# Latent scores wholly in row tiles: nine rounds of four 32-row products for four key tiles, instead of one such round and eight full products

## The chip, the cores and the metric

The kernel runs on one core of a Trainium2 chip. The metric is the time of one execution on the device in microseconds (us). The core has TensorE (PE, its weight loads shown apart as PEld), VectorE (DVE), ScalarE (ACT), GpSimd (POOL) and SyncE (SP), which issues nearly all DMAs here. Each engine takes its instructions in the order in which the program lists them for it.

## The reference

One layer of a transformer, 2048 positions of width 1024, all in float32, one sequence:

```python
z = rms_norm(x) @ w_in                       # q_A, k_A, v_A, c_q, c_kv, k_rope
o_A = windowed attention (8 heads of 64, 2 kv heads, |i-j| <= 128, bias, sink)
# latent attention, 8 heads, all 2048 keys:
q = rms_norm(c_q) @ w_qb                     # per head 64 plain + 32 rotary columns
k, v = rms_norm(c_kv) @ w_kvb                # per head 64 plain columns of k, 64 of v
s = (einsum('bqhd,bkhd->bhqk', qn, k_nope)
     + einsum('bqhr,bkr->bhqk', qr, k_rot)) * scale      # k_rot is shared by all heads
o_B = softmax(s) @ v
x = x + concat(rms_norm(o_A), rms_norm(o_B)) @ w_o
x = x + expert_choice_ffn(rms_norm(x))       # 16 experts, 256 rows each, 3 matrices of 1024 x 1024
```

The change concerns `s` of the latent attention: per head a product over 64 + 32 = 96 rows.

## The kernel before, in words

The program has three regions. Region 1 projects the rows, norms and rotates them and writes queries and keys transposed into DRAM (`qT`, `kT`), each as two parts: a value rounded to the short form that TensorE takes in one pass, and the rest. Region 2 is the attention, region 3 the output projection, the router and the experts.

A score is the sum of three part products, high x high, high x rest and rest x high, so 3 x 96 = 288 rows. Before, that is laid out as two full products of 128 rows (256 rows: `kk[:, 0]` and `kk[:, 1]`, filled by `fetch_k`, L325) and one product of 32 rows for what is left, which is the rotary part that all heads share (`kr`, filled by `fetch_kr`, L337). Four of these 32-row products, for four key tiles, go to the four row groups of the array at once (`rotary`, L1113): that is the one round of before. The queries are laid out to match in `qq` of three slabs (`fetch_qq`, L345).

Region 2 runs over 8 heads, 4 chunks of 512 queries per head, and 4 groups of four key tiles per chunk: `head` (L1097). In each group one round and eight full products write four PSUM banks, two `sb` pairs out of three. ScalarE takes the exponential of each pair into `pp` (L1130, four buffers), VectorE adds it to a sum (L1133, L1135), and two value products per pair, for the two column halves of the array, add to `pv` (L1140). A value step is the two products of one pair. The windowed attention of 16 row tiles is mixed into the same queues: scores at L1004, bias add at L1009, exponential at L1012, values at L1021, denominators at L1043. Its queries come by `fetch_q` (L314), its keys by `fetch_ka` (L319).

The order of each engine's instructions is made when the program is built. Each operation has a cost, needs and a priority; a planner (`Plan.schedule`, L147) runs through them and puts the ready one with the lowest priority next. Priorities are a base plus an offset by stage and engine, the table `OFF2` for region 2. For TensorE it prefers, within 4.0, an operation of the array mode it is in: "r" for row groups, "c" for column halves, none for the full array. Every load is one operation of SP with cost 0.5 (`load`, L409), however many DMAs its function issues; its bytes are counted at 230 KB per us. Keys of the next head and queries of the next chunk are fetched into second buffers. A DMA reuses one of eight semaphores in turn, so it waits until the DMA eight before it has landed. At the end of region 1 SP issues what the start of region 2 needs: the bias table, the windows' first tiles, the first queries (`qq0`) and the first eight key tiles of head 0 (`PRE_K`).

Of the kernel before, what the change touches and what calls it, by code (L numbers as in the profile page):

```python
# [46 lines left out]
OFF2 = {'bfP': -89.2, 'aG': -6.5, 'awV': -1.5, 'bfS': -57.7, 'bfV': 89.2, 'asP': -33.4, 'awP': -84.8, 'bfA': -1.0, 'bfG': -6.1, 'bvP': 29.3, 'awS': -37.9, 'avP': 28.4, 'afS': 47.0, 'blS': -30.5, 'bV': 10.7, 'pfS': 58.5}  # L47
# [211 lines left out]
def build(tc, nc, a, out, dbg=None, upto=9, path="both"):  # L259
# [35 lines left out]
    class Views:  # L295


        def __init__(self):
# [4 lines left out]
            self.qq0 = carve(3, 512)  # L303
            self.va = f(carve(4, 2, 64))
            self.qs = [carve(8, P), None]
            self.kr = carve(4, P)
            v0, k0 = f(carve(NT, VD)), carve(2, SEQ)
            self.free = WB[:, carve.used[0]:]
            v1, k1 = f(carve(NT, VD)), carve(2, SEQ)
# [15 lines left out]
        def fetch_k(self, h, c0, c1):  # L325

            kk, src = f(self.kk[h % 2]), kT[h // 4, :, h % 4]
            cs = slice(c0, c1)
# [106 lines left out]
    def region1():  # L435
        with ExitStack() as st:
# [401 lines left out]
            if PRE_K:  # L838
                pl.load(P * 6144, V2.fetch_qq(0, 0, lambda: V2.qq0), sum((KT[t] for t in range(4)), [MK]), [], pr=PRE_PR + 1)
                pl.load(P * 8 * PRE_K * P, V2.fetch_k(0, 0, PRE_K * P), sum((KT[t] for t in range(PRE_K)), [MK]), [], pr=PRE_PR + 2)  # L840
                pl.load(P * 512 * PRE_K // 4, V2.fetch_kr(0, PRE_K // 4), sum((KT[t] for t in range(PRE_K)), [MK]), [], pr=PRE_PR + 2)
# [20 lines left out]
    def region2(mix):  # L862
# [3 lines left out]
        with ExitStack() as st:  # L866
# [211 lines left out]
            def latent():  # L1078
                vts = [pl.fixed(b) for b in V2.vts]
                KR = pl.fixed(V2.kr)  # L1080
                pl.home.update({("kk", i): V2.kk[i] for i in range(2)})
                pl.home[("qq", 0)] = V2.qq0
                for h in range(8):
                    pl.prio, pl.stage = 64 * h - 20, "bl"
                    kk = pl.buf(wk, [P, 2, SEQ], F32R, "kk", 2)
                    vt = vts[h % 2]
                    cuts = [PRE_K, NT] if h == 0 else [0, 8, NT]
                    if h == 0:
                        kk.slot, kk.t = 0, V2.kk[0]
                        pl.load(P * 512, V2.fetch_kr(PRE_K // 4, 4), [], [(KR, m) for m in range(PRE_K // 4, 4)])  # L1090
                    for c0, c1 in zip(cuts, cuts[1:]):
                        pl.load(P * 1024 * (c1 - c0), V2.fetch_k(h, c0 * P, c1 * P), [], [(kk, kt) for kt in range(c0, c1)])
                        pl.load((c1 - c0) << 15, V2.fetch_v(h, c0, c1), [], [(vt, kt) for kt in range(c0, c1)])
                    for qc in range(4):
                        head(h, qc, kk, vt, KR)

            def head(h, qc, kk, vt, KR):  # L1097
                qsl = slice(qc * 512, qc * 512 + 512)
                pl.prio, pl.stage = 64 * h + 16 * qc - 20, "bl"
                qq = pl.buf(wk, [P, 3, 512], F32R, "qq", 2)  # L1100
                if h + qc == 0:
                    qq.slot, qq.t = 0, V2.qq0
                else:
                    pl.load(P * 6144, V2.fetch_qq(h, qc, qq), [], [qq])
# [3 lines left out]
                for m in range(4):  # L1108
# [636 lines left out]
```

## Time and profile before

| | |
|---|---|
| median of 3 runs | 2641.65 us (2641.4 to 2643.09) |
| profiled execution | 2643.56 us, span of its instructions 2641.8 us |
| mean granted TensorE clock | 0.967 |
| region 2 on TensorE | from 491.58 us (first window scores) to 1220.5 us; output projection from 1229.29 us |
| TensorE, VectorE, ScalarE busy | 94%, 62%, 46% of the span |

The profile lists instructions by line of the program, engine and operation, with the tile they write and the tiles they read. A matmul's record begins when it enters the array; ends are modelled and overlap, so the pace is read from one start to the next. Time in which an engine waits stands behind a row in brackets, with what ended it. A DMA's row on SP is its issue; its data land later.

### The profile page before, as it was taken

How to read it: one execution, taken by the hardware profiler on the slowest of the kernel's cores; microseconds unless marked ns; L12 is line 12 of the kernel's file. 1: busy time of each engine (PE TensorE's matmuls, PEld its weight loads, DVE VectorE, ACT ScalarE, POOL GpSimd, SP SyncE). 2: the span in 40 equal slices, each digit the busy share in tenths (PEclk: the TensorE clock that was granted, in tenths of full speed). 3: DMA queues.
4: the chain of work that ended last, by engine and by line, in shares of the span. 5: the costliest groups of instructions: out<-in, count | busy, mean ns of one | idle time of the engine just before them, and what ended most of it. 6: DMA issues, size and time to landing. Idle time of an engine off the chain costs nothing.

```text
span 2641.8 us, 38721 instructions
## 1 busy us (share of the span) xinstructions
PE 2479.2 (94%) x15002; PEld 1975.9 (75%) x15002; DVE 1645.4 (62%) x3022; ACT 1204.5 (46%) x1731; POOL 343.1 (13%) x284
## 2 busy tenths in 40 slices
PE   6599999699999999998999499999999999999997
PEld 5599999444444444444888399999999999999996
DVE  6366665486768677667767775555555555555552
ACT  5254444344444444444444244545544544554442
POOL 2132333111211111000000000000000000000000
PEclk8799999799999999999999599999999999999999
DMA  5434443864424432314544156666666666666662
GB/s 186 83 110 116 127 113 111 207 158 103 114 75 114 105 81 70 90 53 147 191 160 172 46 168 208 218 212 211 205 223 219 207 212 224 209 207 216 222 193 63
DMA packets 356777, 406.22 MB, mean 154 GB/s; under 512 B 42560, under 2 KB 298432, under 8 KB 356584
## 3 DMA queue, kind: packets, MB, share of 16 engines
q1 hardware_dynamic: 347368, 369.83, 46.0%
q0 software_dynamic: 9216, 33.82, 5.1%
q8 instruction: 121, 1.98, 0.3%
q14 instruction: 72, 0.59, 0.1%
HBM read 318.52 MB, written 85.07 MB: 153 GB/s over the span
## 4 chain that ended last, share of the span: by engine, by line
PE 83%; DVE 6%; DMA 4%; issue 3%; POOL 1%; ACT 1%; SPq 1%; POOLq 0%; DVEq 0%; ACTq 0%
PE y L1660 13%; PE gu L1634 9%; PE gu L1635 9%; PE gu L1636 9%; PE sb L1125 9%; PE u L643 8%; PE pv L1140 7%; PE y L1359 6%; PE u L737 3%; PE sb L1116 2%; PE sb L1043 1%; PE tr L1610 1%; PE tr L813 1%; PE sb L1004 1%; DMA kA<-th 1%
## 5 line engine op out<-in xcount | busy, mean ns | idle before, releaser
L416 DVE TENSOR_TENSOR wlo<-raw,whi 128x2048 fp32r<-128x2048 f32 x192 | 440.0, 2292 | 364.6 <-ACT whi L414 364.6
L1634 PE MATMUL gu<-xh,whi 128*128 128x256 f32 x2048 | 580.6, 283 | 0.0
L1635 PE MATMUL gu<-xl,whi 128*128 128x256 f32 x2048 | 574.8, 281 | 0.0
L1636 PE MATMUL gu<-xh,wlo 128*128 128x256 f32 x2048 | 574.5, 281 | 0.0
L414 ACT ACTIVATE whi<-raw 128x2048 fp32r<-128x2048 f32 x192 | 368.1, 1917 | 277.3 <-PE gu L1635 151.0
L1130 ACT ACTIVATE pp<-sb 128x1024 f32<-128x1024 f32 x256 | 252.4, 1025 | 301.6 <-PE sb L1125 258.2
L1634 PEld LDWEIGHTS gu<-xh,whi 128*128 128x128 f32 x2048 | 385.8, 188 | 0.6
L1635 PEld LDWEIGHTS gu<-xl,whi 128*128 128x128 f32 x2048 | 385.7, 188 | 0.7
L1636 PEld LDWEIGHTS gu<-xh,wlo 128*128 128x128 f32 x2048 | 385.7, 188 | 0.0
L1135 DVE TENSOR_TENSOR acc<-acc,pp 128x1024 f32<-128x1024 f32 x192 | 249.2, 1298 | 124.1 <-ACT pp L1130 114.7
L1660 PE MATMUL y<-whi,aa 128*128 128x512 f32 x1024 | 278.4, 391 | 0.0
L1140 PE MATMUL pv<-pp,WB 128*64 128x512 f32 x1024 | 251.7, 604 | 0.0
L643 PE MATMUL u<-WB,xh 128*128 128x384 f32 (+1 forms) x1024 | 223.2, 340 | 5.1 <-ACT vv L762 2.8
L1660 PEld LDWEIGHTS y<-whi,aa 128*128 128x128 f32 x1024 | 191.3, 188 | 40.5
L643 PEld LDWEIGHTS u<-WB,xh 128*128 128x128 f32 x1024 | 173.9, 192 | 7.3 <-ACT vv L762 3.5
L1359 PE MATMUL y<-whi,aa 128*128 128x512 f32 x512 | 148.8, 402 | 11.0 <-ACT aa L414 8.8
L1660 PE MATMUL y<-wlo,aa 128*128 128x512 f32 x512 | 158.5, 391 | 0.0
L1140 PEld LDWEIGHTS pv<-pp,WB 128*64 128x64 f32 x1024 | 63.9, 136 | 121.8 <-issue 91.5
L1668 POOL DMA_INDIRECT out_dram<-ot,idx x32 | 50.7, 1584 | 793.2 <-ACT ot L1665 759.8
L1125 PE MATMUL sb<-WB 128*128 128x512 f32 x512 | 141.6, 416 | 0.0
L1125 PE MATMUL sb<-qq,WB 128*128 128x512 f32 x512 | 138.1, 411 | 0.0
L643 PE MATMUL u<-WB,xl 128*128 128x336 f32 (+1 forms) x512 | 127.5, 330 | 0.0
(267 smaller groups left out, 3498.0 us busy)
## 6 DMA issues: line engine op xcount, KB each, us to landing
raw<-w_gate SPq DMA_DIRECT2D x64, 1024.0 KB, 4.9
raw<-w_up SPq DMA_DIRECT2D x64, 1024.0 KB, 5.6
raw<-w_down SPq DMA_DIRECT2D x64, 1024.0 KB, 4.9
xt<-x SPq DMA_DIRECT2D x32, 512.0 KB, 4.3
kT<-th SPq DMA_DIRECT2D x30, 384.0 KB, 3.5
qT<-th SPq DMA_DIRECT2D x30, 384.0 KB, 3.2
WB<-kT SPq DMA_DIRECT2D x32, 256.0 KB, 6.2
oT_d<-fo SPq DMA_DIRECT2D x64, 128.0 KB, 2.5
```

What stands on the lines that cost most here:

```text
L414: self.A(n, lambda: act.activation(hi(), src(), AF.Copy, scale=sc()), r + list(rs), [w_hi], need, pr, sb)
L416: self.V(n, lambda: dve.tensor_sub(lo(), src(), f(hi())), r + [w_hi], [w_lo], need, pr)
L643: pe.matmul(z[i]()[:, :n], lh()[:, k % 4, :], rh()[:, k, c0 + i * n:c0 + (i + 1) * n], start=first, stop=last)
L1125: pe.matmul(s()[:, j], kk()[:, c, ksl], qq()[:, c], start=False, stop=c == 1)
L1130: pl.A(1024, lambda s=s, p=p: act.activation(p(), s(), AF.Exp), [s], [p])
L1135: pl.V(1024, lambda p=p: dve.tensor_add(acc(), acc(), p()), [p], [acc])
L1140: pe.matmul(pv()[64 * j:64 * j + 64], vt()[:, 2 * n + j], p()[:, j], start=n == 0, stop=n == 7)
L1359: pe.matmul(pw[i](), o4(l)[:, ks], r_()[:, c:c + 512], start=first, stop=last_)
L1634: pe.matmul(o, c3(hi, ND)[:, k, fs], xh()[:, k], start=k == 0, stop=False)
L1635: pe.matmul(o, c3(hi, ND)[:, k, fs], xl()[:, k], start=False, stop=False)
L1636: pe.matmul(o, c3(lo, ND)[:, k, fs], xh()[:, k], start=False, stop=k == ND - 1)
L1660: pe.matmul(y[i][j](), l()[:, ts], r_()[:, o:o + 512], start=first, stop=last_)
```

## The change

All 288 rows of a score go through row groups. The 96 rows of each part are cut into three slabs of 32: `kk` holds six slabs per head (three of the high part, three of the rest), four key tiles side by side on the four row groups; `qq` holds the same six slabs of the queries, each on all four row groups. For a group of four key tiles `ROUNDS` lists nine pairs of slabs, and each round is four products of 32 rows, for the four key tiles, which add to the four banks: 36 products of 32 rows in place of 4 of 32 and 8 of 128. The separate rotary buffer and the operation for it are gone, and the group's nine rounds are one operation of the planner. A half head of keys is fetched by 24 DMAs of 32 rows x 2 x 512 bytes in place of four, a chunk of queries by eight DMAs with 1.5 MB in place of 0.75 MB. Both exponentials of a group now follow the whole operation. The table OFF2 has other offsets and five more entries.

```diff
-OFF2 = {'bfP': -89.2, 'aG': -6.5, 'awV': -1.5, 'bfS': -57.7, 'bfV': 89.2, 'asP': -33.4, 'awP': -84.8, 'bfA': -1.0, 'bfG': -6.1, 'bvP': 29.3, 'awS': -37.9, 'avP': 28.4, 'afS': 47.0, 'blS': -30.5, 'bV': 10.7, 'pfS': 58.5}
+OFF2 = {'bfP': -89.2, 'aG': -6.5, 'awV': -51.6, 'bfS': 8.6, 'bfV': 91.4, 'asP': -20.8, 'awP': -53.3, 'bfA': -1.0, 'bfG': -6.1, 'bvP': 2.1, 'awS': -37.9, 'avP': 28.4, 'afS': 82.4, 'blS': -10.9, 'bV': 10.7, 'pfS': 58.5, 'aV': -27.4, 'bsP': -8.5, 'bA': -1.8, 'pfA': -10.0}
...
-            self.qq0 = carve(3, 512)
+            self.qq0 = carve(6, 512)
...
-            self.kr = carve(4, P)
-            v0, k0 = f(carve(NT, VD)), carve(2, SEQ)
+            v0, k0 = f(carve(NT, VD)), carve(6, 4, P)
...
-        def fetch_k(self, h, c0, c1):
+        def fetch_k(self, h, m0, m1):
...
             def go():
-                sync.dma_start(kk[0:HD, 0, cs], src[0, :, cs])
-                sync.dma_start(kk[HD:P, 0, cs], src[1, NO:HD, cs])
-                sync.dma_start(kk[0:NO, 1, cs], src[0, 0:NO, cs])
-                sync.dma_start(kk[NO:P, 1, cs], src[1, 0:NO, cs])
-            return go
-
-        def fetch_kr(self, m0, m1):
-
-            def go():
-                src = kT[0, 0, 0, NO:HD].rearrange("d (m j s) -> d j m s", j=4, s=P)
-                for j in range(4):
-                    sync.dma_start(f(self.kr)[RD * j:RD * j + RD, m0:m1], src[:, j, m0:m1])
+                for c in range(6):
+                    part = src[c // 3, RD * (c % 3):RD * (c % 3) + RD].rearrange("d (m j s) -> d j m s", j=4, s=P)
+                    for j in range(4):
+                        sync.dma_start(kk[RD * j:RD * j + RD, c, m0:m1], part[:, j, m0:m1])
             return go
...
-                sync.dma_start(q[0:HD, 0], src[0])
-                sync.dma_start(q[HD:P, 0], src[0, NO:HD])
-                sync.dma_start(q[0:NO, 1], src[1, 0:NO])
-                sync.dma_start(q[NO:P, 1], src[0, 0:NO])
                 for j in range(4):
-                    sync.dma_start(q[RD * j:RD * j + RD, 2], src[1, NO:HD])
+                    for c in range(2):
+                        sync.dma_start(q[RD * j:RD * j + RD, 3 * c:3 * c + 3], src[c].rearrange("(a d) s -> d a s", d=RD))
...
-                    def rotary(pairs=pairs, m=m):
-                        for j in range(4):
-                            rows = slice(RD * j, RD * j + RD)
-                            pe.matmul(pairs[j // 2][0]()[:, j % 2], V2.kr[rows, m], qq()[rows, 2], start=True, stop=False)
-
-                    pl.mm(1.5 * U, rotary, [(KR, m), qq], [b for b, _ in pairs] + [order], need=[b for _, b in pairs] + [pv], mode="r")
+                    def score(pairs=pairs, m=m):
+                        for n, (c, d) in enumerate(ROUNDS):
+                            for j in range(4):
+                                rows = slice(RD * j, RD * j + RD)
+                                pe.matmul(pairs[j // 2][0]()[:, j % 2], kk()[rows, c, m], qq()[rows, d], start=n == 0, stop=n == 8)
+
+                    pl.mm(9 * U, score, [(kk, m), qq], [b for b, _ in pairs], need=[b for _, b in pairs] + [pv], mode="r")
                     for i, (s, p) in enumerate(pairs):
-                        for j in range(2):
-                            kt = 4 * m + 2 * i + j
-
-                            def score(s=s, j=j, ksl=slice(kt * P, kt * P + P)):
-                                for c in range(2):
-                                    pe.matmul(s()[:, j], kk()[:, c, ksl], qq()[:, c], start=False, stop=c == 1)
-
-                            pl.prio, pl.stage = base + 2 * i + j, "bs"
-                            pl.mm(2 * U, score, [(kk, kt), qq], [s, order])
...
+            ROUNDS = [(c, d) for c in range(6) for d in ((c, 3 + c) if c < 3 else (c - 3,))]
```

The change moves instructions on SP at the start of region 2. Before, behind the query loads of the second chunk (`qq_5575`) and ahead of the queries of window 1 (`qs_5548`) SP's queue holds eight key DMAs of head 1 (L331 to L334):

```order
L1053 DMA es_5551<-a_sink 128x8
L331 DMA WB<-kT 96x1024
L332 DMA WB<-kT 32x1024
L333 DMA WB<-kT 64x1024
L334 DMA WB<-kT 64x1024
L359 DMA WB<-v_62 128x8x64
L331 DMA WB<-kT 96x1024
L332 DMA WB<-kT 32x1024
L333 DMA WB<-kT 64x1024
L334 DMA WB<-kT 64x1024
L359 DMA WB<-v_62 128x8x64
L314 DMA qs_5548<-qA 64x8x128 x2
```

In the changed kernel, from the branch into region 2 on (`qq_5634` are the second chunk's queries, `qs_5564` those of window 1):

```order
L1685 COMPARE_AND_BRANCH
L332 DMA WB<-kT 32x2x128 x24
L346 DMA WB<-v_62 128x8x64
L342 DMA qq_5634<-qT 32x3x512 x8
L1039 DMA es_5567<-a_sink 128x8
L332 DMA WB<-kT 32x2x128 x24
L346 DMA WB<-v_62 128x8x64
L332 DMA WB<-kT 32x2x128 x24
L346 DMA WB<-v_62 128x8x64
L313 DMA qs_5564<-qA 64x8x128 x2
```

The loads stand in the same order, but 48 key DMAs of head 1 and 24 of head 0 now stand ahead of the window's queries behind the branch, and 24 more of head 0 ahead of the branch.

On TensorE the place is the first use of those window queries. Before (L1116 a round, L1125 full products, L1140 values, L1004 window scores):

```order
L1116 MATMUL sb_5735<-qq_5575,WB 128x512 x2
L1116 MATMUL sb_5736<-qq_5575,WB 128x512 x2
L1125 MATMUL sb_5735<-qq_5575,WB 128x512 x4
L1125 MATMUL sb_5736<-qq_5575,WB 128x512 x4
L1140 MATMUL pv_5601<-pp_5704,WB 64x512 x2
L1140 MATMUL pv_5739<-pp_5737,WB 64x512 x2
L1116 MATMUL sb_5766<-qq_5575,WB 128x512 x2
L1116 MATMUL sb_5767<-qq_5575,WB 128x512 x2
L1125 MATMUL sb_5766<-qq_5575,WB 128x512 x4
L1004 MATMUL sb_5780<-qs_5548,WB 128x512 x4
L1125 MATMUL sb_5767<-qq_5575,WB 128x512 x4
L1140 MATMUL pv_5739<-pp_5738,WB 64x512 x2
```

In the changed kernel (L1101 the rounds, here the last two of the second chunk's first group, L990 window scores, L1116 values, L1007 window values):

```order
L1101 MATMUL sb_5908<-qq_5634,WB 128x512 x2
L1101 MATMUL sb_5909<-qq_5634,WB 128x512 x2
L1101 MATMUL sb_5908<-qq_5634,WB 128x512 x2
L1101 MATMUL sb_5909<-qq_5634,WB 128x512 x2
L990 MATMUL sb_5954<-qs_5564,WB 128x512 x4
L990 MATMUL sb_5965<-qs_5564,WB 128x512 x4
L1116 MATMUL pv_5912<-pp_5910,WB 64x512 x2
L1116 MATMUL pv_5912<-pp_5911,WB 64x512 x2
L990 MATMUL sb_5980<-qs_5564,WB 128x512 x4
L1007 MATMUL pv_5956<-pp_5955,WB 64x512 x2
```

The window's first scores stood inside the second group of the second chunk and stand behind its first group now, with the values of that group behind them.

Further on, where before two value steps follow each score group, the changed order alternates one and three of them. A place from a later chunk of the changed kernel (the last rounds of one group, `sb_9025` and `sb_9026`; a value step, the sum `pv_8807` of the chunk before; the first rounds of the next group):

```order
L1101 MATMUL sb_9025<-qq_8717,WB 128x512 x2
L1101 MATMUL sb_9026<-qq_8717,WB 128x512 x2
L1116 MATMUL pv_8807<-pp_8966,WB 64x512 x2
L1101 MATMUL sb_9073<-qq_8717,WB 128x512 x2
L1101 MATMUL sb_9074<-qq_8717,WB 128x512 x2
```

One value step stands between the two groups; the first group's own two are issued behind the second, with the first step of the second's.

## Rows read from the trace of the kernel before

**Rows 1.** The page: shares of the span, and the chain by line.
```profile
PE 2479.2 (94%) x15002; PEld 1975.9 (75%) x15002; DVE 1645.4 (62%) x3022; ACT 1204.5 (46%) x1731; POOL 343.1 (13%) x284
...
PE y L1660 13%; PE gu L1634 9%; PE gu L1635 9%; PE gu L1636 9%; PE sb L1125 9%; PE u L643 8%; PE pv L1140 7%; PE y L1359 6%; PE u L737 3%; PE sb L1116 2%; PE sb L1043 1%; PE tr L1610 1%; PE tr L813 1%; PE sb L1004 1%; DMA kA<-th 1%
```
**Rows 2.** Busy us of each engine by stretch, then granted clock, DMA share, GB/s.
```profile
491.00:510.00 19.00, 5.23 (x12) 3.33 (x12) 2.71 (x3) 1.51 (x2) 0.00 (x0) 0.50 0.96 245
...
640.00:660.00 20.00, 20.00 (x93) 9.29 (x91) 11.29 (x11) 10.44 (x11) 0.00 (x0) 1.00 0.16 47
```
**Rows 3.** Timeline of TensorE, steady stretch: start us, us, what, tiles, count.
```profile
642.73 0.51 PE L1116 MATMUL sb<-qq,WB 32*128 32x512 f32 x4
643.17 2.13 PE L1125 MATMUL sb<-qq,WB 128*128 128x512 f32 x8
645.24 1.94 PE L1140 MATMUL pv<-pp,WB 128*64 128x512 f32 x8
647.10 0.50 PE L1116 MATMUL sb<-qq,WB 32*128 32x512 f32 x4
```
**Rows 4.** Timeline of TensorE: runs of four and of twelve full products.
```profile
570.91 1.20 PE L1004 MATMUL sb<-WB 128*128 128x512 f32 x4
572.04 1.94 PE L1021 MATMUL pv<-pp,WB 128*64 128x512 f32 x8
...
595.20 3.04 PE L1004 MATMUL sb<-WB 128*128 128x512 f32 x12
598.16 1.08 PE L1021 MATMUL pv<-pp,WB 128*64 128x512 f32 x4
```
**Rows 5.** Timeline of TensorE: a run of sixteen value records.
```profile
1012.51 3.65 PE L1140 MATMUL pv<-pp,WB 128*64 128x512 f32 x16
1016.10 0.51 PE L1116 MATMUL sb<-qq,WB 32*128 32x512 f32 x4
```
**Rows 6.** Timeline of the weight loads: those of eight full products.
```profile
1016.53 1.69 PEld L1125 LDWEIGHTS sb<-qq,WB 128*128 128x128 f32 x8 [0.25 <-DMA WB<-qT]
```
**Rows 7.** Timeline of ScalarE: a group's two exponentials.
```profile
644.41 1.96 ACT L1130 ACTIVATE pp<-sb 128x1024 f32<-128x1024 f32 x2 [2.41 <-DVE am L1151]
```
**Rows 8.** DMAs of two lines: issue ns min/median/max; us to landing.
```profile
L342 SPq DMA_DIRECT2D WB<-kT x8: 425/428/1067, 493.4 to 509.7; - x8
...
L314 SPq DMA_DIRECT2D qs<-qA x16: 573/616/1118, 527.0 to 975.7; - x16
DMA to landing us min/median/max: 3.7/4.4/9.9
```
**Rows 9.** Timeline of SP's issues, start of region 2.
```profile
481.57 2.98 SPq L350 DMA_DIRECT2D WB<-qT  x1
493.41 1.99 SPq L342 DMA_DIRECT2D WB<-kT  x4
496.40 0.46 SPq L711 DMA_DIRECT2D kA<-th  x1
507.47 2.62 SPq L342 DMA_DIRECT2D WB<-kT  x4
527.00 1.97 SPq L314 DMA_DIRECT2D qs<-qA  x2
529.60 3.90 SPq L314 DMA_DIRECT2D WB<-qA  x1
```
**Rows 10.** Timeline of TensorE at the start; the wait and what ended it.
```profile
509.57 0.79 PE L1116 MATMUL sb<-WB 32*128 32x512 f32 x2 [9.49 <-ACT pp L1012]
510.29 3.48 PE L1125 MATMUL sb<-WB 128*128 128x512 f32 x8
538.43 1.16 PE L1004 MATMUL sb<-qs,WB 128*128 128x512 f32 x4 [0.18 <-DMA qs<-qA]
550.72 1.92 PE L1021 MATMUL pv<-pp,WB 128*64 128x512 f32 x4 [3.55 <-ACT pp L1012]
```
**Rows 11.** Timeline of TensorE: short products of the router, each with a load.
```profile
1494.74 0.57 PE L1530 MATMUL gu<-s,ones 128*128 128x32 bf16 x16
```

More of the change, by code (lines that the diff above doesn't have):

```diff
@@ L302, in __init__ @@
             self.KK = {n: kk[:, :4 * n * P].rearrange("p (c s) -> p c s", c=4) for n in (4, 6)}
-            self.qq0 = carve(3, 512)
+            self.qq0 = carve(6, 512)
             self.va = f(carve(4, 2, 64))
             self.qs = [carve(8, P), None]
-            self.kr = carve(4, P)
-            v0, k0 = f(carve(NT, VD)), carve(2, SEQ)
+            v0, k0 = f(carve(NT, VD)), carve(6, 4, P)
             self.free = WB[:, carve.used[0]:]
-            v1, k1 = f(carve(NT, VD)), carve(2, SEQ)
+            v1, k1 = f(carve(NT, VD)), carve(6, 4, P)
             self.vts, self.kk = [v0, v1], [k0, k1]
@@ L838, in region1 @@
             if PRE_K:
-                pl.load(P * 6144, V2.fetch_qq(0, 0, lambda: V2.qq0), sum((KT[t] for t in range(4)), [MK]), [], pr=PRE_PR + 1)
-                pl.load(P * 8 * PRE_K * P, V2.fetch_k(0, 0, PRE_K * P), sum((KT[t] for t in range(PRE_K)), [MK]), [], pr=PRE_PR + 2)
-                pl.load(P * 512 * PRE_K // 4, V2.fetch_kr(0, PRE_K // 4), sum((KT[t] for t in range(PRE_K)), [MK]), [], pr=PRE_PR + 2)
+                pl.load(P * 12288, V2.fetch_qq(0, 0, lambda: V2.qq0), sum((KT[t] for t in range(4)), [MK]), [], pr=PRE_PR + 1)
+                pl.load(P * 768 * PRE_K, V2.fetch_k(0, 0, PRE_K // 4), sum((KT[t] for t in range(PRE_K)), [MK]), [], pr=PRE_PR + 2)
                 pl.load(PRE_K * P * 256, V2.fetch_v(0, 0, PRE_K), sum((KT[t] for t in range(PRE_K)), [MK]), [], pr=PRE_PR + 3)
@@ L1079, in latent @@
                 vts = [pl.fixed(b) for b in V2.vts]
-                KR = pl.fixed(V2.kr)
                 pl.home.update({("kk", i): V2.kk[i] for i in range(2)})
@@ L1084, in latent @@
                     pl.prio, pl.stage = 64 * h - 20, "bl"
-                    kk = pl.buf(wk, [P, 2, SEQ], F32R, "kk", 2)
+                    kk = pl.buf(wk, [P, 6, 4, P], F32R, "kk", 2)
                     vt = vts[h % 2]
@@ L1089, in latent, with head @@
                         kk.slot, kk.t = 0, V2.kk[0]
-                        pl.load(P * 512, V2.fetch_kr(PRE_K // 4, 4), [], [(KR, m) for m in range(PRE_K // 4, 4)])
                     for c0, c1 in zip(cuts, cuts[1:]):
-                        pl.load(P * 1024 * (c1 - c0), V2.fetch_k(h, c0 * P, c1 * P), [], [(kk, kt) for kt in range(c0, c1)])
+                        pl.load(P * 768 * (c1 - c0), V2.fetch_k(h, c0 // 4, c1 // 4), [], [(kk, m) for m in range(c0 // 4, c1 // 4)])
                         pl.load((c1 - c0) << 15, V2.fetch_v(h, c0, c1), [], [(vt, kt) for kt in range(c0, c1)])
                     for qc in range(4):
-                        head(h, qc, kk, vt, KR)
-            def head(h, qc, kk, vt, KR):
+                        head(h, qc, kk, vt)
+            def head(h, qc, kk, vt):
                 qsl = slice(qc * 512, qc * 512 + 512)
                 pl.prio, pl.stage = 64 * h + 16 * qc - 20, "bl"
-                qq = pl.buf(wk, [P, 3, 512], F32R, "qq", 2)
+                qq = pl.buf(wk, [P, 6, 512], F32R, "qq", 2)
                 if h + qc == 0:
@@ L1103, in head @@
                 else:
-                    pl.load(P * 6144, V2.fetch_qq(h, qc, qq), [], [qq])
+                    pl.load(P * 12288, V2.fetch_qq(h, qc, qq), [], [qq])
                 pv = pv_()
@@ L1166, in region2 @@
             fin = []
-            order = pl.fixed(None)
+            ROUNDS = [(c, d) for c in range(6) for d in ((c, 3 + c) if c < 3 else (c - 3,))]
             PB = 4
```

1 line of the change is left out of this document (removed).

## The prediction

> **What bounds the kernel now.** I read the page's shares and chain first [rows 1]: TensorE is busy for 94% of the span, and nearly every line of the chain that ended last is its work; the latent attention stands in it with its scores (sb L1125 9%, sb L1116 2%) and values (pv L1140 7%). Then the table by stretches [rows 2]. From 640 to 660 us TensorE has no idle time at all, while ScalarE is busy for 10.4 us of the 20 and VectorE for 11.3: there a group costs what TensorE needs for it. From 491 to 510 us it is the other way round: TensorE works 5.2 of 19 us, at a granted clock of 0.50 (1.2 GHz), and the DMA engines are 96% busy. Attention starts there, on data that SP has to fetch. The two stretches are priced apart.
>
> The timeline of TensorE in the steady stretch [rows 3] gives the unit: round of four 32-row products at 642.73, eight full products from 643.17, values from 645.24, next round at 647.10. A group of four key tiles is 2.51 us of scores and 1.86 us of values, and there are 8 heads x 4 chunks x 4 = 128 groups.
>
> **The change part by part.** *Scores.* Removed: eight full products and one round per group; added: nine rounds. The price of a full product in a run comes from two runs of the same shape [rows 4]: four take 570.91 to 572.04 = 1.13 us, twelve take 595.20 to 598.16 = 2.96 us, so each further one costs 1.83 / 8 = 0.229 us, and the first, with its uncovered load and the drain behind it, 1.13 - 3 x 0.229 = 0.44 us. The round of four in rows 3 takes 643.17 - 642.73 = 0.44 us as well: alone, four 32-row products cost what one full product costs, so their loads and streams do run beside each other. Nine rounds in one run then take 0.44 + 8 R. No row shows two rounds in a row, so R is bounded. Below: the values work in two column halves, with loads of their own; eight take 1.86 us in rows 3 and sixteen 3.59 us [rows 5], so eight more cost 1.73 us, 0.216 us for 512 columns: R = 0.216. Above: if each round paid its load and drain again, R = 0.44. I take R = 0.229, the nearest row: same columns, same type, a new load each, and the eight loads of such a run take 1.69 us [rows 6], within the 2.1 us of its eight products, under the streaming. Scores then take 0.44 + 1.83 = 2.27 us, 0.24 less than 2.51; x 128 = 30.7 us. Of this some 3 us go back: 14 runs of windowed scores now follow a round directly, and where before full products followed full products they now pay an entry, 0.44 - 0.229 = 0.21 us each. Net gain 28 us (lower end R = 0.216: 41; upper end R = 0.44: a loss of 186 + 3).
>
> The Trainium skill (TensorE: Matmul & The Clock Gate, Part 3, What overlaps and what doesn't) says that a weight load overlaps running matmuls only when it goes to other row groups, and (Measured speedup vs the span model) that four 32-row products of 512 columns gain 3.07 times. The second would make R 0.229 x 4 / 3.07 = 0.30 and the score group 2.83 us. Rows 3 show four products in the 0.44 us of one, and rows 6 show covered loads to the same row groups, so for full products the trace disagrees with the first; for rounds in a row no row here decides.
>
> *The activations.* All four banks of a group now finish together; before, the first pair finished after four products, and its exponential ran beside the other four. Two take 1.96 us [rows 7]. The first will now begin about when the values begin (the second one does so now: 644.41 + 1.96 - 1.03 = 645.34 against 645.24) and free its pair 1.0 us later, while the next score group needs two of three pairs. The planned order often puts a single value step between two score groups; alone it takes about 1.0 us, so the wait is 0 to 0.15 us on half of the groups: 0 to 10 us. I take 1 us.
>
> *SP's queue.* Keys of a half head were four large DMAs and are now 24 of 32 rows; queries stay at eight per chunk with twice the bytes. A small key DMA (L342 of before) is issued in 0.43 us [rows 8], four in a row take 1.99 us [rows 9], so 0.43 to 0.50 each; I take 0.47. A head's 48 hold SP for 22.6 us. In the steady stretch the queries two chunks ahead stand behind them. From the end of a chunk's scores: query DMAs 5 us, keys until 28, four more DMAs until 30, next queries issued by 35 and landed by 38; they are needed two chunks later, 2 x (4 x 2.27 + 8 x 0.93) = 33 us plus one value run (2) and, in most heads, one window (7), 35 to 42 us. This is hidden but for the head without windows: 1 us, and 3 to 6 per head (six of them) if every issue takes a tenth longer.
>
> *The start.* Here nothing hides it. TensorE's queue in both programs reaches the first window that needs fetched queries after about five groups. Before, it started at 538.43 us, 0.18 us after its data were awaited [rows 10]; the DMAs for it went out at 527.00 [rows 9]. Between SP's first query DMA (481.57) and those stood 54 DMAs and now stand 126, 96 of them small key DMAs. Step by step: first queries, twice 0.75 MB at the 245 GB/s of rows 2, 3 us more, so keys from about 492 to 504 (lanes wait for the queries, then 0.47 us each); nine stores of the last row tile, 11 us before on full queues (496.40 to 507.47 [rows 9]), then about 0.6 us each, to 510; 24 keys to 521.5; values, eight queries, one small, to 528; 48 keys and two values to 552; the window's two to 553.5; landing 4.4 us in the middle (rows 8): 558. The groups before it end at about 539 (the third waits until 524 to 526 for its keys), so TensorE stands for 19 us, and at 558 it has done half a score group (1.2 us) and one value step (0.9) less than before at 538.4. That is 22 us late. Behind so long a wait the clock will be down: after the 9.49 us wait before 509.57 a run of eight products took 3.48 us instead of 2.1 (rows 10), so add 2. Back comes the wait of 3.55 us at 550.72 [rows 10], for exponentials of windows that are by then long done. Start: +20 us (from 12, if lanes and issue run at their shortest, to 27).
>
> *Sum* on the profiled execution, 2643.56 us: -28 + 1 + 1 + 20 = -6 us, 2637.6. The median of the runs shown is 1.9 us under that execution, so 2635.7 us for the median. Behind attention TensorE is the bound again (rows 1), so the shift passes on whole; I let the wait before the output projection stay as it is, since it is for the last heads' way through DRAM.
>
> **The rivals.** *Rounds that don't cover their loads (slower).* Place: the 36 loads of a group. For it: each round reloads the very row groups that stream, and the value rows can be read the other way, two halves side by side, a pair each 0.43 us, as long as a lone round. Against it: rows 6, and the pace of short products, 16 with a load each in 0.57 us [rows 11], so four loads and products are issued in 0.14 us. It decides at R = 0.235: there the scores' gain no longer pays for the start. With half of the load and drain uncovered, R = 0.33: 128 x (0.44 + 2.64 - 2.51) = +73, +3 +22: 2740; with a tenth, R = 0.25: -9 + 3 + 22 = +16, 2658. By the Trainium skill's 3.07 times it would be 41 + 3 + 22 = +66, 2708. Chance 0.19.
>
> *SP starves the heads (slower).* The block of 48 costs 3 to 6 us in each of six heads instead of 1 in all: +18 to 36, 2653 to 2670. For it: 22.6 us of keys, 32 query DMAs at about 0.5 us, stores and windows make some 50 us of issue for some 82 us of head (16 x 4.13 us and two windows), in a queue that also waits for stores; against it: the sum above leaves 2 to 5 us of room. Chance 0.11.
>
> *The start is cheaper.* Half of the 54 DMAs of before were slowed by full queues (one issue of 3.90 us [rows 9]); freer queues give 10 to 12 us late instead of 20: 2626. Chance 0.13.
>
> *No change.* The exponentials take their 10 us on the groups with one value step between, or the start costs its upper 27: 2640 to 2645. Chance 0.15.
>
> **How the numbers follow.** My forecast, scores at R from 0.216 to 0.229 and a start of 16 to 24 us, has 0.42 and spans 2618 to 2640 (41 instead of 28 and 16 instead of 20 below, 24 above). What a measurement of this kernel can tell from no change is about 0.2%, 5.3 us. Of the forecast's 0.42, 0.29 lie more than that below 2641.65; with the cheaper start's 0.13 faster has 0.42. Same: 0.13 of the forecast and 0.14 of the fourth rival: 0.27. Slower: 0.19 + 0.11 and 0.01 of the fourth: 0.31. The range goes from 2615 (R = 0.216 with a start of 12) to 2668 (heads starved, or R = 0.25 to 0.26); it leaves out the larger half of the first rival, the worst heads of the second, and a start that costs nothing.
>
> **What would show it.** Right: score groups of 2.2 to 2.3 us between the first load and the values; single value steps between groups with under 0.15 us idle; key DMAs 0.47 us apart in blocks of 24 and 48; a wait of 15 to 20 us on TensorE near 540 us that ends with the window's queries; heads that end about 30 us nearer to their start in all. Wrong: rounds 0.25 us or more apart; waits for qq at the head of a chunk behind each key block; a start on time. If the total falls by 20 us or more, it is the start that I priced too high; if it rises by 15 or more, the rounds.

## The result, and the profile after

The changed kernel takes 2685.07 us in the median of four runs (2683.69 to 2688.16), the kernel before, beside it, 2641.53 us. The ratio is 1.0168 with a 95% interval of 1.0155 to 1.018: 43.5 us slower, outside the range that I gave. The profiled execution has a span of 2684.0 us at a mean granted clock of 0.957.

Region 1 is the same work in both and differs by up to 5 us between the profiled executions (its last transposes start at 488 to 493 us over all runs of this study; 489.49 before, 492.99 now), so I compare region 2 alone, from the last transposes on TensorE to the first product of the output projection: 739.8 us before, 780.9 us now, 41.1 us more.

The page, the shares and the chain by line, which answer to [rows 1]:

```profile
PE 2474.8 (92%) x18074; PEld 2006.0 (75%) x18074; DVE 1657.3 (62%) x3022; ACT 1201.0 (45%) x1731; POOL 344.8 (13%) x284
...
PE y L1636 13%; PE sb L1101 11%; PE gu L1610 9%; PE gu L1611 9%; PE gu L1612 9%; PE u L630 9%; PE pv L1116 8%; PE y L1335 6%; PE u L724 3%; PE sb L990 2%; DVE acc L1111 1%; PE sb L1029 1%; PE tr L1586 1%; PE pv L1007 1%; PE tr L800 1%
```

TensorE works 4.4 us less than before: the time went into waits. In region 2 it stands still for 85.1 us (40.7 before). The timeline of TensorE in a steady stretch of the changed kernel answers to [rows 3] (start us, us, engine, line, tiles, count):

```profile
688.29 2.38 PE L1101 MATMUL sb<-qq,WB 32*128 32x512 f32 x36
690.60 1.08 PE L1116 MATMUL pv<-pp,WB 128*64 128x512 f32 x4
691.61 2.54 PE L1101 MATMUL sb<-qq,WB 32*128 32x512 f32 x36
694.08 2.80 PE L1116 MATMUL pv<-pp,WB 128*64 128x512 f32 x12
```

A group of nine rounds takes 690.60 - 688.29 = 2.31 us, or 2.47 us where a single value step stands ahead of it (the group from 691.61). By the sum of the prediction the first is 0.44 + 8 R, so R = 0.234 us, where I had taken 0.229. The loads are covered.

What changed most is the start, on SP and on TensorE. SP's issues in the changed kernel, which answer to [rows 9]:

```profile
485.24 10.40 SPq L342 DMA_DIRECT2D WB<-qT  x8
496.34 13.29 SPq L332 DMA_DIRECT2D WB<-kT  x24
...
510.21 0.53 SPq L698 DMA_DIRECT2D kA<-th  x1
...
520.43 0.42 SPq L698 DMA_DIRECT2D qA<-WB  x1
521.01 13.04 SPq L332 DMA_DIRECT2D WB<-kT  x24
...
539.94 14.76 SPq L332 DMA_DIRECT2D WB<-kT  x24
554.75 0.43 SPq L346 DMA_DIRECT2D WB<-v  x1
555.23 11.53 SPq L332 DMA_DIRECT2D WB<-kT  x24
566.80 0.43 SPq L346 DMA_DIRECT2D WB<-v  x1
567.27 1.27 SPq L313 DMA_DIRECT2D qs<-qA  x2
```

The waits of TensorE at the start of region 2, which answer to [rows 10]:

```profile
502.15 9.69 PE L1101 MATMUL sb<-WB 32*128 32x512 f32 x36 [8.74 <-DMA WB<-kT]
...
547.30 4.54 PE L1101 MATMUL sb<-WB 32*128 32x512 f32 x36 [8.69 <-ACT pp L1106]
...
573.02 3.75 PE L990 MATMUL sb<-qs,WB 128*128 128x512 f32 x8 [15.29 <-DMA qs<-qA]
```

Window 1's queries are issued at 567.27 us (527.00 before) and TensorE starts on them at 573.02 (538.43 before), after a wait of 15.29 us. The waits of TensorE over region 2, by line and releaser (total us, times, longest), show two more that were not there:

```profile
PE sb L1029 <- ACT pp L998: 19.5, 10, 2.0
...
PE sb L1101 <- DMA WB<-qT: 5.7, 4, 2.1
```

The sums L1029, which need a bank pair, wait ten times for the exponential of a window. And at 1146 us a score group waits for the queries of its own chunk. SP's row ahead of them is the key block of the last head:

```profile
1112.48 28.36 SPq L332 DMA_DIRECT2D WB<-kT  x48
```

Its 48 key DMAs took 28.36 us, and the query DMAs went out at 1142.67. No window is left there to give SP time: the last window scores run at 1089 us.

### The profile page after: what moved, and what is told of

Read it like the earlier page. It is cut to its first block, busy times and chain, and to the rows that moved or that the text cites. A ratio compares the mean times of both kernels' runs of the same rounds, so it can differ in the third digit from the quotient of the medians.

```text
span 2684.0 us, 45144 instructions
## 1 busy us (share of the span) xinstructions
PE 2474.8 (92%) x18074; PEld 2006.0 (75%) x18074; DVE 1657.3 (62%) x3022; ACT 1201.0 (45%) x1731; POOL 344.8 (13%) x284
## 4 chain that ended last, share of the span: by engine, by line
PE 85%; DVE 6%; DMA 3%; ACT 2%; issue 2%; SPq 1%; POOL 1%; POOLq 0%; DVEq 0%; ACTq 0%
PE y L1636 13%; PE sb L1101 11%; PE gu L1610 9%; PE gu L1611 9%; PE gu L1612 9%; PE u L630 9%; PE pv L1116 8%; PE y L1335 6%; PE u L724 3%; PE sb L990 2%; DVE acc L1111 1%; PE sb L1029 1%; PE tr L1586 1%; PE pv L1007 1%; PE tr L800 1%
## 5 line engine op out<-in xcount | busy, mean ns | idle before, releaser
L1111 DVE TENSOR_TENSOR acc<-acc,pp 128x1024 f32<-128x1024 f32 x192 | 261.1, 1360 | 91.4 <-ACT pp L1106 83.1
L1116 PE MATMUL pv<-pp,WB 128*64 128x512 f32 x1024 | 255.9, 612 | 0.9 <-ACT pp L1106 0.5
L1101 PEld LDWEIGHTS sb<-WB 32*128 32x128 f32 x2304 | 122.8, 188 | 93.9 <-issue 42.7
L1101 PE MATMUL sb<-WB 32*128 32x512 f32 x2304 | 168.1, 412 | 23.4 <-DMA WB<-kT 8.7
L1101 PEld LDWEIGHTS sb<-qq,WB 32*128 32x128 f32 x2304 | 116.3, 185 | 64.8 <-issue 32.5
L1116 PEld LDWEIGHTS pv<-pp,WB 128*64 128x64 f32 x1024 | 65.1, 138 | 129.6 <-issue 101.0
L1101 PE MATMUL sb<-qq,WB 32*128 32x512 f32 x2304 | 156.7, 405 | 0.9 <-ACT pp L1106 0.9
```

Of the source, the lines that this page charges most:

```text
L1101: pe.matmul(pairs[j // 2][0]()[:, j % 2], kk()[rows, c, m], qq()[rows, d], start=n == 0, stop=n == 8)
L1111: pl.V(1024, lambda p=p: dve.tensor_add(acc(), acc(), p()), [p], [acc])
L1116: pe.matmul(pv()[64 * j:64 * j + 64], vt()[:, 2 * n + j], p()[:, j], start=n == 0, stop=n == 7)
```

## The experiments

Ratios are against the kernel before, run beside each. Line numbers shift by one or two between the kernels. Times by stretch and by region are those of one profiled execution of each run.

### Two causes tried alone, and the rounds

**Eight key DMAs** (e1). The key tiles are stored in DRAM in the order of the fetch, so that one DMA carries three slabs:

```diff
-                for c in range(6):
-                    part = src[c // 3, RD * (c % 3):RD * (c % 3) + RD].rearrange("d (m j s) -> d j m s", j=4, s=P)
-                    for j in range(4):
-                        sync.dma_start(kk[RD * j:RD * j + RD, c, m0:m1], part[:, j, m0:m1])
+                for a in range(2):
+                    for j in range(4):
+                        cols = slice(512 * j + P * m0, 512 * j + P * m1)
+                        sync.dma_start(kk[RD * j:RD * j + RD, 3 * a:3 * a + 3, m0:m1].rearrange("p b m s -> p b (m s)"),
+                                       src[a, :, cols].rearrange("(b d) s -> d b s", d=RD))
...
-                        pl.load(HD * 4096, lambda th=th, dst=dst, i=i: sync.dma_start(
-                            dst[i, :, :, :, rows].rearrange("c h d s -> d (c h) s"), f(th()).rearrange("d c h s -> d (c h) s")), [th], note(KT[t]))
+                        at = slice(P * (4 * (t % 4) + t // 4), P * (4 * (t % 4) + t // 4) + P) if dst is kT else rows
+                        pl.load(HD * 4096, lambda th=th, dst=dst, i=i, at=at: sync.dma_start(
+                            dst[i, :, :, :, at].rearrange("c h d s -> d (c h) s"), f(th()).rearrange("d c h s -> d (c h) s")), [th], note(KT[t]))
```

> Changed kernel, but a half head of keys comes by 8 DMAs of 32 rows x 3 x 256 columns instead of 24 (the key tiles lie in DRAM in the order in which they are fetched). Theory 1, SP's queue at the start and behind the key blocks costs the 43 us: 64 DMAs fewer at about 0.55 us stand ahead of window 1's queries, so these land near 540 instead of 573 us, the wait of 15.3 us on TensorE goes and so does the late query load of the second last head (8 us); total 2685 - 35 - 8 = 2640 (2632 to 2650). Theory 2, the start is late because the bytes are (queries twice as large, full DMA queues): 2675 to 2685. Theory 3, the order of the planner and the sums' waits cost it: within 5 us of 2685.

Measured: 2641.62 us, ratio 1.0008 (0.9999 to 1.0018). The orders, the bytes and the rounds are those of the changed kernel; the number of key DMAs is not, nor the size of their pieces in DRAM (1 KB instead of 512 bytes). SP's issues:

```profile
512.21 5.38 SPq L332 DMA_DIRECT2D WB<-kT  x8
...
524.33 6.20 SPq L332 DMA_DIRECT2D WB<-kT  x8
530.57 0.43 SPq L347 DMA_DIRECT2D WB<-v  x1
531.05 4.74 SPq L332 DMA_DIRECT2D WB<-kT  x8
535.83 0.44 SPq L347 DMA_DIRECT2D WB<-v  x1
536.31 1.27 SPq L313 DMA_DIRECT2D qs<-qA  x2
```

A block of keys holds SP for 4.7 to 6.2 us instead of 11.5 to 14.8 here, window 1's queries go out 31 us earlier, and region 2 takes 736.7 us, 44.2 less. Of that 32.2 us are gained up to the first sums of latent heads (L1029 in one, L1031 in the other, counted from the last transposes: 110.5 and 78.3 us), 10.4 in the half head at 1146 us, whose queries are now in time. Theory 1 holds; that twice the bytes of queries or the order make the start late has fallen.

**24 key DMAs in the kernel before** (e4). The other side of the same question:

```diff
+            cuts = [cs.start, cs.start + 3 * P, cs.start + 6 * P, cs.stop]
+
...
-                sync.dma_start(kk[0:HD, 0, cs], src[0, :, cs])
-                sync.dma_start(kk[HD:P, 0, cs], src[1, NO:HD, cs])
-                sync.dma_start(kk[0:NO, 1, cs], src[0, 0:NO, cs])
-                sync.dma_start(kk[NO:P, 1, cs], src[1, 0:NO, cs])
+                for p0, c, a, r0, n in ((0, 0, 0, 0, 3), (HD, 0, 1, NO, 1), (0, 1, 0, 0, 2), (NO, 1, 1, 0, 2)):
+                    for i in range(n):
+                        for k0, k1 in zip(cuts, cuts[1:]):
+                            sync.dma_start(kk[p0 + RD * i:p0 + RD * i + RD, c, k0:k1], src[a, r0 + RD * i:r0 + RD * i + RD, k0:k1])
```

> Kernel before, with one edit: the four key DMAs of a half head are cut into 24 (32 rows x 384 or 256 columns); same bytes, full products, old table. Theory 1, the number of key DMAs on SP's queue is the loss: window 1's queries leave some 60 DMAs x 0.55 = 33 us later, TensorE waits about 25 us near 540 us, total 2641.5 + 30 = 2672 (2662 to 2690). Rival, rounds and order cost it: within 8 us of 2641.5.

Measured: 2668.03 us, ratio 1.0102 (1.0084 to 1.012). TensorE's first row on window 1's queries:

```profile
566.82 2.05 PE L1006 MATMUL sb<-qs,WB 128*128 128x512 f32 x4 [9.28 <-DMA qs<-qA]
```

Full products, the old table, the same bytes in pieces of 1 KB and more, and still the window starts 28 us later than before (27 counted from the last transposes): the number of DMAs is enough for it.

**Full products in the changed kernel** (e3). SP's queue and all orders stay, only the nine rounds go. These products do not add up to the reference's scores; the run is there for its time (so are e5 and e9):

```diff
-                        for n, (c, d) in enumerate(ROUNDS):
-                            for j in range(4):
-                                rows = slice(RD * j, RD * j + RD)
-                                pe.matmul(pairs[j // 2][0]()[:, j % 2], kk()[rows, c, m], qq()[rows, d], start=n == 0, stop=n == 8)
+                        for j in range(4):
+                            rows = slice(RD * j, RD * j + RD)
+                            pe.matmul(pairs[j // 2][0]()[:, j % 2], kk()[rows, 0, m], qq()[rows, 0], start=True, stop=False)
+                        for j in range(4):
+                            for c in range(2):
+                                pe.matmul(pairs[j // 2][0]()[:, j % 2], kk()[:, 1 + c, m], qq()[:, 1 + c], start=False, stop=c == 1)
```

> Changed kernel, but each group's nine rounds are one round and eight full products of 128 rows on the same buffers (the scores are then not the reference's). SP's queue and every order stay. If a round costs what a full product costs (0.233 us, read from the changed kernel's trace), a group goes from 2.31 to 2.51 us and the total by 128 x 0.2 = 25 us, less what lies under waits at the start, to 2708 (2702 to 2712). If rounds gain nothing over full products (uncovered loads, stalls in the rounds): 2680 to 2690.

Measured: 2676.47 us, ratio 1.0137 (1.012 to 1.0154), 8.6 us *less* than with the rounds. My expectation failed. Region 2 is 1.5 us shorter, the rest lies in regions 1 and 3, whose code is the same; why they differ is open, and a median can hide a few us of region 2 behind them. So the 0.18 us that each group gains are spent again. The stretches between two sums of latent heads show on what (stretch, its length, busy us of PE, PEld, DVE, ACT, POOL, then granted clock, DMA share, GB/s); the changed kernel first:

```profile
759.29:802.89 43.60, 41.63 (x384) 21.42 (x384) 33.14 (x25) 19.67 (x22) 6.87 (x3) 1.00 0.62 141
802.89:848.20 45.31, 43.35 (x385) 21.76 (x385) 32.72 (x25) 19.69 (x22) 6.88 (x3) 0.96 0.54 113
```

and with full products:

```profile
756.85:801.29 44.44, 42.67 (x193) 20.15 (x193) 33.68 (x25) 19.89 (x22) 6.87 (x3) 1.00 0.64 141
801.29:845.72 44.43, 42.67 (x193) 20.14 (x193) 33.68 (x25) 19.88 (x22) 6.87 (x3) 1.00 0.56 112
```

With rounds such a half head is 0.84 us shorter in one case and 0.88 us longer in the next: after its wait of 1.97 us the granted clock fell to 0.50 (1.2 GHz) there. The timeline of TensorE in the changed kernel shows it in the four products behind the wait, 1.93 us where they take 1.08 at full clock; the last row is the stretch, with its granted clock as the third figure from the end:

```profile
802.89 1.33 PE L1029 MATMUL sb<-am,ones 128*64 128x512 f32 x4 [1.97 <-ACT pp L998]
804.00 1.93 PE L1007 MATMUL pv<-pp,WB 128*64 128x512 f32 x4
805.71 1.67 PE L1116 MATMUL pv<-pp,WB 128*64 128x512 f32 x4
...
804.00:805.50 1.50, 1.50 (x6) 0.49 (x4) 1.14 (x1) 0.67 (x1) 1.34 (x1) 0.50 1.16 211
```

That happened behind four of the ten waits with rounds (1.94 to 1.97 us, those of the other six as long) and behind none of the ten with full products (1.75 to 1.76 us). It costs some 1.7 us each time (45.31 - 43.60). The other places where the rounds lose are the start (2.5 us more up to the first sums of latent heads, 110.5 against 108.0) and the half head that waits for its queries (45.3 against 43.3).

**The old table** (e2): `OFF2` of the kernel before in the changed kernel, nothing else.

> Changed kernel with the offset table OFF2 of the kernel before; rounds and 24 DMAs per half head stay. If the order by the new table (one and three value steps, sums behind a score group) costs the 12 us of waits before the sums L1029, these waits fall from 23.7 to about 11 us and the time to about 2672 (2665 to 2678). If SP's 24 DMAs decide alone: 2680 to 2690. If the new table is what makes the rounds bearable: above 2695.

Measured: 2739.03 us, ratio 1.0375 (1.0357 to 1.0394). The waits of TensorE:

```profile
PE sb L1101 <- DMA WB<-qT: 24.0, 18, 3.4
PE sb L990 <- DMA qs<-qA: 22.1, 3, 14.6
PE sb L1101 <- ACT pp L998: 19.7, 1, 19.7
```

With the old order each of the last four heads waits for queries behind the key block (at 963, 1042, 1123 and 1203 us): it is the picture of my second rival, which the new table avoids in all heads but one. The windows show how: with the old table their last scores run at 884 us and the heads behind have none, with the new one at 1089. The new table is not part of the loss, it keeps it smaller. **The old table with eight key DMAs** (e10) separates the two:

> Eight key DMAs with the offset table of the kernel before. With 24 DMAs that table cost 54 us against the new one. If this was SP's queue (46 us of waits for query DMAs there), nearly all of it goes here: 2642 + 10 = 2652 (2640 to 2665). If the table's order on TensorE is worse by itself: above 2675.

Measured: 2659.65 us, ratio 1.007 (1.0053 to 1.0087). 79 of 97 us go with the DMAs; 18 us against the new table are the order's own.

### What the rounds are worth

**Full products with eight key DMAs** (e5, the edits of e1 and e3 together):

> The kernel with eight key DMAs per half head, but with one round and eight full products in place of the nine rounds (scores then not the reference's); same order on every engine. It measures what the rounds bring where SP no longer decides. By the group times (2.31 against 2.49 us, a quarter of the rounds' groups stalled to 2.45) rounds gain 0.14 x 128 = 18 us: 2659 (2652 to 2666). If the waits before the sums and the slower clock behind them, which the run with full products on the changed kernel did not show, eat the gain: 2636 to 2648.

Measured: 2641.89 us, ratio 1.0008 (0.9999 to 1.0018), the same as with rounds. Region 2 takes 740.9 us against 736.7, so 4.2 us are left of the gain; the medians show none of it (regions 1 and 3 differ by as much, see e3).

**The windows' additions on VectorE** (e6). Why do the sums wait? The exponential that they need comes late, because its bias addition is late on VectorE. There, in the changed kernel:

```profile
752.77 3.36 DVE L1111 TENSOR_TENSOR acc<-acc,pp 128x1024 f32<-128x1024 f32 x1
756.16 0.69 DVE L1130 TENSOR_TENSOR fo<-pv,fu 64x512 f32<-64x512 f32 x1
756.88 1.23 DVE L995 TENSOR_TENSOR sb<-sb,WB 128x1024 f32<-128x1024 f32 x1
```

and on GpSimd at the same time:

```profile
752.67 2.37 POOL L1000 TENSOR_TENSOR acw<-pp,pp 128x1024 f32<-128x1024 f32 x1 [30.18 <-ACT pp L998]
```

The addition L1111 takes 1.22 us at 751.45 and 3.36 us when GpSimd's addition begins just before it. The Trainium skill (GPSIMD Engine Reference, Specifications) says that GpSimd shares its memory interfaces with VectorE and contends with instructions of two SBUF inputs there; these rows agree. The edit, on the kernel with eight key DMAs (e1) and at the same place of the program order:

```diff
-                        pl.G(1024, lambda p=p, q=prev: pool.tensor_add(acc(), q(), p()), [prev, p], [acc])
+                        pl.G(1024, lambda p=p, q=prev: dve.tensor_add(acc(), q(), p()), [prev, p], [acc])
...
-                        pl.G(1024, lambda p=p: pool.tensor_add(acc(), acc(), p()), [p], [acc])
+                        pl.G(1024, lambda p=p: dve.tensor_add(acc(), acc(), p()), [p], [acc])
```

> The kernel with eight key DMAs per half head, with the windows' 30 additions of two probability tiles (acw) on VectorE instead of GpSimd, at the same place of the program order. Theory: VectorE's addition of latent probabilities takes 3.36 instead of 1.22 us where GpSimd's addition runs beside it (2.37 us), that makes the next window's bias addition 2.1 us late, and the sums behind it wait 1.95 us for the bank, after which the clock falls in some. Then the waits before the sums fall from 1.95 to about 1 us or less, the clock does not fall, and the time goes from 2641.6 to 2622 (2612 to 2630). Rival, the wait is the order's own (bank taken by the window just ahead): within 4 us of 2641.6.

Measured: 2626.85 us, ratio 0.9944 (0.9926 to 0.9962), faster than the kernel before. The timeline of VectorE there:

```profile
849.76 1.23 DVE L1002 TENSOR_TENSOR acw<-pp,pp 128x1024 f32<-128x1024 f32 x1
850.90 1.22 DVE L1113 TENSOR_TENSOR acc<-acc,pp 128x1024 f32<-128x1024 f32 x1
852.15 0.69 DVE L1132 TENSOR_TENSOR fo<-pv,fu 64x512 f32<-64x512 f32 x1
852.88 1.23 DVE L997 TENSOR_TENSOR sb<-sb,WB 128x1024 f32<-128x1024 f32 x1
```

and that of TensorE, two sums of latent heads and their waits:

```profile
855.28 1.08 PE L1031 MATMUL sb<-am,ones 128*64 128x512 f32 x4 [0.80 <-ACT pp L1000]
...
897.77 1.08 PE L1031 MATMUL sb<-am,ones 128*64 128x512 f32 x4 [0.82 <-ACT pp L1000]
```

Two additions one after the other on VectorE take 2.4 us where the one beside GpSimd took 3.4; the sums wait 0.8 us, the clock stays at 1.00, and every half head with windows takes 42.4 to 42.5 us (897.77 - 855.28) in place of 43.6 and 45.3.

**The same with full products** (e9, the edit of e3 on e6):

> Eight key DMAs, additions on VectorE, but one round and eight full products in place of nine rounds (scores then not the reference's). With the 1.95 us waits and the slow clock behind them gone on both sides, the rounds' own worth shows. From group times (0.18 us less, half of the groups stalled by 0.14): 0.1 x 128 = 14 us, so 2627 + 14 = 2641 (2636 to 2646). If rounds are worth nothing in the whole: 2624 to 2630; if their full 0.18 x 128 = 23 us: 2650.

Measured: 2631.65 us, ratio 0.9968 (0.9955 to 0.998). Its sums follow each other by 896.64 - 853.34 = 43.30 us:

```profile
853.34 1.08 PE L1031 MATMUL sb<-am,ones 128*64 128x512 f32 x4 [0.62 <-ACT pp L1000]
...
896.64 1.08 PE L1031 MATMUL sb<-am,ones 128*64 128x512 f32 x4 [0.62 <-ACT pp L1000]
```

Rounds gain 0.8 to 0.9 us per half head with windows; over region 2 that leaves 730.8 - 723.8 = 7.0 us, 4.8 in the medians. The two regions as a whole, e6 first (stretch, its length, busy us of PE, PEld, DVE, ACT, POOL, then granted clock, DMA share, GB/s):

```profile
493.41:1217.21 723.80, 676.57 (x6130) 350.24 (x6129) 537.62 (x444) 316.96 (x340) 33.84 (x16) 0.97 0.60 131
...
489.82:1220.62 730.80, 689.46 (x3059) 325.14 (x3057) 542.81 (x444) 319.88 (x340) 33.68 (x16) 0.97 0.61 129
```

With rounds TensorE works 12.9 us less and stands still for 5.9 us more (47.2 against 41.3). This is below what I expected; 2.8 us are lost before the first sums of latent heads.

**The additions moved in the kernel before** (e8, the edit of e6 on it):

> Kernel before (full products, four key DMAs, old table) with the windows' 30 additions on VectorE at the same place of the order. It tells whether the 14 us of the run with the additions moved belong to the new order. Theory: the kernel before waits only 6.8 us for GpSimd's sum acw and 4.7 us for window exponentials, so it gains at most half of the 11.5: 2639.5 - 3 = 2636 (2632 to 2643). Rival, the moved additions help any order alike: 2625 (2620 to 2630).

Measured: 2643.33 us, ratio 1.0015 (1.0006 to 1.0025): no gain. The gain of e6 belongs to the new order, in which the sums stand behind a score group with a window's exponential due; full products gain in that order too (2641.89 us in e5, 2631.65 in e9).

**Two attempts on the order.** In e7 the planner knows of the moved additions (`pl.V` in place of `pl.G`):

> As the run before, but the planner knows that the additions are VectorE's, so the order changes: most sums then stand behind a value step instead of behind a score group. If the sums' waits of 1.95 us and the clock behind them are what is left of the loss, nearly all of them go: 2641.6 - 10 x 1.95 - 6 x 1.7 + 1 = 2613 (2606 to 2625). Rival, VectorE's 37 us more become the bound in windows: 2635 to 2655.

Measured: 2650.83 us, ratio 1.0042 (1.0028 to 1.0056). The sums' wait for the window's exponential went as expected (1.5 us left of 8.1), but others came in its place, of window values for exponentials and of three sums for the moved additions:

```profile
PE pv L1009 <- ACT pp L1000: 14.6, 13, 3.4
PE sb L1031 <- DVE acw L1004: 9.7, 3, 4.0
```

Region 2 takes 748.4 us against 723.8 in e6, more than these waits. The rival of the expectation, that VectorE becomes the bound in windows, has the number, but nothing here tests it.

In e11 both value steps of a group are one operation, so that score groups and value runs alternate:

```diff
-                        pl.prio, pl.stage = base + 4 + 2 * i + 1.5, "bv"
-                        pl.mm(4 * U, value, [p, (vt, 2 * n), (vt, 2 * n + 1)], [pv], mode="c")
+                        if i == 1:
+
+                            def value(m=m, ps=[b for _, b in pairs]):
+                                for n, p in zip((2 * m, 2 * m + 1), ps):
+                                    for j in range(2):
+                                        pe.matmul(pv()[64 * j:64 * j + 64], vt()[:, 2 * n + j], p()[:, j], start=n == 0, stop=n == 7)
+
+                            pl.prio, pl.stage = base + 5.5, "bv"
+                            pl.mm(8 * U, value, [b for _, b in pairs] + [(vt, kt) for kt in range(4 * m, 4 * m + 4)], [pv], mode="c")
```

> Eight key DMAs, additions on VectorE, and both value steps of a group as one operation of the planner, so that score groups and whole value runs alternate in place of one and three steps. If the 0.14 to 0.16 us by which every second score group is longer (2.45 instead of 2.30) is the wait for the bank pair that the first exponential frees behind a single value step, every group takes 2.3 us and half a head without windows goes from 34.9 to 34.4 us; in total 2626.85 - 5 = 2622 (2615 to 2628), less or more by where windows come to stand. Rival, the longer groups have another reason (loads of the rounds after values): 34.9 us stays, 2624 to 2632.

Measured: 2628.64 us, ratio 0.9953 (0.9936 to 0.9969). Its last heads, without windows:

```profile
1126.87 2.37 PE L1103 MATMUL sb<-qq,WB 32*128 32x512 f32 x36
1129.17 1.94 PE L1120 MATMUL pv<-pp,WB 128*64 128x512 f32 x8
1131.04 2.37 PE L1103 MATMUL sb<-qq,WB 32*128 32x512 f32 x36
```

Seven of eight groups take 2.30 us there (one, the second behind the sums, 2.52), and half a head 34.4 us where e6 has 35.1 (sums at 1137.26 and 1172.33 us). So the 0.15 us of every second group are the wait for the second bank pair behind a single value step. Where windows stand the new order waits elsewhere, half heads with windows take 43.5 us and more in place of 42.4, and the total is no better.

## Why the prediction was wrong

The steps of its sum against region 2 (41.1 us more), each by the runs that separate it:

| step | predicted | measured | by |
|---|---|---|---|
| rounds, net of what follows them | -28 + 1 | -4 (with the slow clock), -7 without | e1 against e5, e6 against e9 |
| start, behind 72 more DMAs (e1 takes 64 of them away) | +20 | +32 | first sums, changed kernel against e1 |
| SP in the steady heads | +1 | +12 (10.4 of it in one head) | the rest of e1 |
| new order, twice the bytes of queries, eight key DMAs instead of four | 0 | +1 | e5 against before |

**The pace of a round was nearly right.** It is 0.234 us against 0.229: four 32-row products in a run cost here what one full product costs, 0.23 us, and the first rival, uncovered loads, has fallen. With it falls the price by the Trainium skill's figure of 3.07 (TensorE: Matmul & The Clock Gate, Part 3), 2.83 us for a group that takes 2.31. But 0.234 us is also where the prediction's own sum has no gain left (0.235). My sentence that a rise of 15 us or more would be the rounds was wrong too.

**The start was the right mechanism, mis-sized.** I had window 1's queries land at 558 us; it was 573. Of these 15 us 3.5 are not the start's: region 1 ended that much later in this execution, the first query DMAs went out at 485.24 instead of 481.57 us, and so the keys began at 496 instead of 492. The rest is two stages: the nine stores took 10.8 us (510.21 to 521.01), as long as before, where I had assumed that freer queues would shorten them to 6 (5 us); and the 96 key DMAs were issued in 13.29 + 13.04 + 14.76 + 11.53 = 52.6 us, 0.55 us each, where I took 0.47 from a run of four (some 6 us). Counted from the last transposes the window starts at 80.0 us, before at 48.9, 31 us later where the sum has 20. My third rival, a cheaper start, was on the wrong side of the sum.

**SP starves one head.** The second rival was priced for six heads at 3 to 6 us; the new order avoids it in all but one, which costs 10.4 us, of which 5.7 are the waits and most of the rest the slow clock behind them (granted clock 0.50 from 1149 to 1155 us). It is the head without windows, for which the sum has 1 us: it left no room there, and the 48 key DMAs took 28.36 us instead of 22.6. The old table shows the rival whole (e2).

**The rounds' gain was too large from the start, and was given back in part.** The group is 2.31, not 2.27 us, and the full products that it replaces take 2.49 in the middle of all groups (e9), not 2.51: 0.18 us gained, not 0.24, which is some 8 us over 128 groups. Of these groups 36 (e6) are 0.1 to 0.2 us longer for a bank pair, which I had bounded at 10 us and taken as 1: 6 us in all. And the sums wait, which no term had: 23.7 us in all against 11.6 before. Most of that is the order's, for with full products they wait 21.3 us in it (e5); what the rounds add is 2 us of waiting and the slow clock behind four of the waits, 1.7 us each. I had read the order at two and three places for what stands behind the score groups, but not asked where the sums stand: they need a third bank pair, and the one operation that now takes two pairs at once leaves it to the window ahead.

So it was no single rival: the start went beyond its own upper bound of 27 us, one head of the second rival came on top, and the gain that was to pay for it had a quarter of its size at most.

That the new order as such costs 1 us is a net: its sums wait longer, while TensorE changes mode less often. How much each of these is was not separated. Nor was why the rounds lose 2.8 us ahead of the first latent sums (79.6 against 76.8 us in e6 and e9), nor what makes up all of the 5.9 us that TensorE stands longer with them.

## What to carry to other kernels

Count the DMAs of a new layout, not its bytes, and lay them along the one queue that issues them up to the first instruction that needs what stands behind: 64 small ones too many cost 32 us here, and storing the tiles in the order of the fetch got these back. A gain per group on a busy engine is worth only what the order lets through: look for each operation that needs a buffer of the same pool, and ask which of its holders is released last. And a short wait can cost twice, by itself and by the clock behind it.

## What the runs showed of the hardware

- 32-row products on four row groups pipeline from round to round as full products do: nine rounds in 2.31 us, loads covered.
- A VectorE addition of two SBUF tiles (128 x 1024, f32) took 3.36 us beside a GpSimd addition of 2.37 us, and 1.22 us without.
- Behind waits of 1.94 to 1.97 us on TensorE in the changed kernel the granted clock fell to 0.50 in four of ten cases (1.7 us lost each time); behind ten of 1.75 to 1.76 us with full products it did not.
- Key DMAs of 32 rows x 2 x 512 bytes were issued 0.48 to 0.62 us apart in blocks of 24 and 48, those of 32 rows x 3 x 1024 bytes 0.59 to 0.84 us apart in blocks of eight.
